# Short-convolution input projection in groups of four column tiles, half of the contraction by seven products of quarters

## The chip, the core and the metric

The kernel runs on one core of a Trainium2 chip. The metric is the device time of one execution, in microseconds (us); the median of three runs is given, and one further execution was taken with the hardware profiler. Engines are named as in the profile: PE is TensorE (matmuls; PEld its weight loads), DVE is VectorE, ACT is ScalarE, POOL is GpSimd, SP is SyncE, which here issues the loads from HBM.

## What is computed

Two layers over 512 latent tokens of width 1024: a mixer and a gated feed-forward part in each, with an adaptive normalisation ahead of both. The part that the change touches is the mixer of the second layer, a short gated convolution; the feed-forward part is shown because its up projection already has the form that the change uses.

```python
def short_conv_mixer(h, w_in, conv_w, conv_b, w_out):
    gate_b, gate_c, u = jnp.split(h @ w_in, 3, axis=-1)
    return (gate_b * dwconv3(gate_c * u, conv_w, conv_b)) @ w_out

def conv_ffn(h, w_up, conv_w, conv_b, w_down):
    a, val = jnp.split(h @ w_up, 2, axis=-1)
    return (jax.nn.gelu(dwconv3(a, conv_w, conv_b), approximate=False) * val) @ w_down

def dwconv3(h, w, b):
    hp = jnp.pad(h, ((0, 0), (1, 1), (0, 0)))
    return hp[:, :-2] * w[0] + hp[:, 1:-1] * w[1] + hp[:, 2:] * w[2] + b
```

`w_in` is 1024 x 3072, so the three outputs `gate_b`, `gate_c` and `u` have 8 column tiles of 128 each, 24 tiles.

## The kernel before

**Layout and precision.** Activations lie transposed: 128 features on the partitions, 512 tokens along the row, 8 such k tiles for a width of 1024. Each fp32 number is used as a high part (a cast to fp32r) and a low part (the rest). ACT casts the high part (`whi`), DVE subtracts it to get the low part (`wlo`), and each product is three matmuls (`mm3`, lines 288 to 290): high by high, high by the activation's low, low by high. One matmul multiplies a 128 x 128 weight block with 512 tokens ("wide") or with half of them ("narrow", 256).

**Weights.** `Weights` holds a plan of loads and of the blocks that are cast from each. `_load` (line 64) gives SP a load of 1 MB into one of two raw buffers `wraw`; `conv` casts the next block in the plan with ACT and DVE (lines 92 and 93, in `_block` lines 125 and 126). The cast blocks rotate through three buffers of 1024 columns, `whi` and `wlo`, so a block waits until the matmuls that read its buffer before are through.

**Quad and pair.** `quad` makes four tiles in two halves of 256 tokens, so that it can start when only the first half of the normalised activations is ready; after the first half's fourth k tile it calls `rest`, which finishes the norm. `pair` makes two tiles with 48 wide matmuls (8 k tiles, 3 each). The mixer's input projection takes a quad for the first c and u tiles and then pairs: b0, c1, u1, b1, c2, and so on to b3, ten pairs. After each pair ACT and DVE do the elementwise part: `cs` is a copy of c (line 1287), c times u (line 1295), the three taps by `conv3` (one ACT product, line 1212, and two DVE operations, lines 1213 and 1214), the product with b (line 1305), and the split into high and low (`mch`, `mcl`, lines 284 and 285) for the output projection `o1`.

**Group.** `group` makes four tiles in the up projections. The contraction's first half (k tiles 0 to 3), the four tiles and the 512 tokens are cut into quarters, and seven products of quarters take the place of eight: the quarters' sums and differences of the weights are made by DVE (`S1` to `S4`, lines 108 to 114), those of the activations once for each projection in `differences` (`T1` to `T4`, lines 1128 to 1138). Products: S1, A11, A12, S2, S3, S4 and A22, 12 narrow matmuls each. The second half of the contraction is done as before with W1 and W2, 24 wide matmuls each. In all 48 wide and 84 narrow. The sum of the products is made in PSUM and, between banks, by copies on ACT (line 1176) and additions on DVE (lines 1181 and 1201). The order of the casts is `QORDER`. S1 and A11 share one `whi`/`wlo` buffer, A12 has one, W1 one, then S2 with S3, S4 with A22, and W2 take the three again. The casts of S1, A11 and A12 of the next group are called behind W2's, that of W1 when the next group has started.

**Units.** The modulation of the second layer (a 1024 x 6144 product with one vector) is done on DVE between the other work: a unit is one `scalar_tensor_tensor` of 128 x 512 on a tile `ar` that SP has loaded (lines 485, 502, 504); after eight units come a reduction (line 508), two small matmuls that gather (`pad`, line 514), and four writes into `mod` (line 520). Three `ar` buffers rotate.

**Order.** The code is written in program order; a scheduler sets each engine's own order at build time, and each engine then takes its instructions strictly in that order, waiting on semaphores. Instructions marked with `pin` (the units among them) keep their order among themselves.

Of the kernel before, what the change touches and what calls it, by code (L numbers as in the profile page):

```python
# [9 lines left out]
F32 = mybir.dt.float32  # L10
# [8 lines left out]
P = 128  # L19
D = 1024  # L20
# [154 lines left out]
def backbone(ctx: ExitStack, tc: tile.TileContext, a, out, dump=None):  # L175
# [23 lines left out]
    def cols(w, c0):  # L199
        return [([ktiled(w)[:, :, c0 : c0 + 256]], [(0, 0, w.shape[0] // P, j, j + P) for j in (0, P)])]  # L200
# [20 lines left out]
    for j in range(4):  # L221
        plan += cols(w_out, 256 * j)

    def ffn_up_plan(l):
        r = cols(up[l], 0) + cols(up[l], FF)
        for j in range(FT // 2 - 1):
            q = [a["upq"][l, j, i][:, None, :] for i in range(2)]
            r += [([q[0]], QORDER), ([q[1]], [])]
        return r

    plan += ffn_up_plan(0)
    for j in range(4):
        plan += [rows_cols(down[0], k0, k1, 256 * j) for k0, k1 in kgroups]
    for j in range(4):
        plan += cols(od_in, D + 256 * j) + cols(od_in, 2 * D + 256 * j) + cols(od_in, 256 * j)
    for j in range(4):
        plan += cols(od_out, 256 * j)
    plan += ffn_up_plan(1)
# [856 lines left out]
    def pair(nm, src):  # L1095

        w = [ws.get(), ws.get()]
        o = [acc_t(f"pp{nm}{i}") for i in range(2)]
        for i in range(2):
            mms(o[i], w[i], src, 0, 0, KT, slice(0, T), True, True)  # L1100
        return o
# [121 lines left out]
    def units(n):  # L1223
        for _ in range(n):
            ada.unit(aux_t)
# [48 lines left out]
        dbg(f"xb{k}", xT[k][:])  # L1274


    mix = []
    for j in range(4):
        if j == 0:
            oc, ou = quad("c", nrm.h, rest)  # L1280
        else:
            oc = pair(f"c{j}", nrm.h)
            units(3)
        cs = []
        for i in range(2):
            t = gp.tile([P, T], F32, tag=f"g{16 + i}", name=f"cs{j}{i}")
            S.copy(t[:], oc[i][:])
            cs.append(t)
        if j:
            ou = pair(f"u{j}", nrm.h)  # L1290
            units(3)
        ts_ = []
        for i in range(2):
            m = 2 * j + i
            V.tensor_tensor(cs[i][:], ou[i][:], cs[i][:], ALU.mult)
            t = fp.tile([P, T], F32, tag="t", name=f"sc{m}", bufs=5)
            conv3(t, cs[i], rowv(76 + m, 1), rowv(84 + m, 1), rowv(92 + m, 1), rowv(68 + m, 1))
            ts_.append(t)
        ob = pair(f"b{j}", nrm.h)
        units(3)  # L1300
        for i in range(2):
            m = 2 * j + i
            mh = gp.tile([P, T], F32R, tag=f"g{2 * m}", name=f"mch{m}")
            ml = gp.tile([P, T], F32R, tag=f"g{2 * m + 1}", name=f"mcl{m}")
            V.tensor_tensor(ob[i][:], ob[i][:], ts_[i][:], ALU.mult)
            split(mh[:], ml[:], ob[i][:])
            mix.append((mh, ml))
    nrm = Norm("f1", 4, (1, 24))
    rest = project_back("o1", mix, [(0, 8)], mod[:, 1, 16:24], nrm)
    for k in range(KT):  # L1310
# [69 lines left out]
_INS = ["ada_w", "ev_w_in", "ev_w_out", "od_w_in", "od_w_out", "ffn_w_up", "ffn_w_down", "final_norm_w"]  # L1380


def layout(inputs):
    arrays = {n: np.ascontiguousarray(inputs[n]) for n in _INS}
    arrays["xT"] = np.ascontiguousarray(np.asarray(inputs["x"])[0].T)
# [2 lines left out]
                                "od_conv_w", "ada_b")]  # L1388
    for l in range(2):
        vecs += [inputs["ffn_conv_w"][l], inputs["ffn_conv_b"][l]]  # L1390
    q = np.asarray(inputs["ffn_w_up"]).reshape(2, KT, P, 2, FT // 2, 2, P)[:, :, :, :, 1:]
    blk = lambda k0, k1, m: q[:, k0:k1, :, :, :, m].transpose(0, 4, 2, 3, 1, 5).reshape(2, FT // 2 - 1, P, -1)
    arrays["upq"] = np.ascontiguousarray(np.stack([
        np.concatenate([blk(0, 2, 1), blk(2, 4, 1), blk(0, 2, 0), blk(2, 4, 0)], -1),
        np.concatenate([blk(4, 8, 0), blk(4, 8, 1)], -1)], 2))
    arrays["vec"] = np.ascontiguousarray(np.concatenate([np.asarray(v).reshape(-1, P) for v in vecs], 0).T)
    rpb = np.asarray(inputs["na_rpb"])[0].reshape(4, 2, 15, 31)
    rp = np.zeros((4, 15, 2, WPAD), rpb.dtype)
# [29 lines left out]
```

## Time and profile before

| | us |
|---|---|
| median of 3 runs | 1335.97 (1333.49 to 1336.93) |
| profiled execution, its own time | 1333.99 |
| its span, first to last instruction | 1332.2 |
| PE, DVE, ACT busy | 1304.5, 965.4, 625.2 |

The span is what the trace shows; 1.8 us of the execution lie around it. A row of the timeline reads: start, duration, engine, line, operation, tile written and tiles read, shape, number, and in brackets how long the engine had been idle before and what ended that. A matmul's duration is longer than the distance to the next one, as they are pipelined; the distance of the starts is what a stream of them costs. The same holds to a small degree for DVE and ACT.

### The profile page before, as it was taken

The numbers are of one execution on the slowest core, as the hardware profiler recorded it, in microseconds if no ns is written. First come the engines' busy times: TensorE is split into PE (matmuls) and PEld (weight loads), VectorE is DVE, ScalarE is ACT, GpSimd is POOL, SyncE is SP. The second block draws the span as 40 slices with busy tenths as digits, with TensorE's granted clock in tenths as the row PEclk, the third lists the DMA queues.
The fourth block names the chain that finished last, engine by engine and source line by source line (L and its number), as shares of the span: only waits on it lengthen the run. The fifth ranks groups of instructions, "written<-read, shape, count | busy, mean of one in ns | idle before, by whom it ended". The sixth has DMA issues, their size and how long they took to land. (4 is left out here: it accounts for less than half of the span.)

```text
span 1332.2 us, 21229 instructions
## 1 busy us (share of the span) xinstructions
PE 1304.5 (98%) x8456; PEld 1147.6 (86%) x8456; DVE 965.4 (72%) x1688; ACT 625.2 (47%) x1085; POOL 84.3 (6%) x87
## 2 busy tenths in 40 slices
PE   7999999999999999999999999999999999999997
PEld 4798888888779998889877898888999989899997
DVE  4668897887778878788766776667789897782333
ACT  4443445555545656565422253223456565663223
POOL 2204332311000000000000000000000000000000
PEclk9999999999999999999999999999999999999999
DMA  9842113674562122323466734555403423242231
GB/s 293 265 123 84 33 33 82 152 182 134 153 206 96 64 99 92 127 71 119 141 211 198 226 132 143 167 165 174 158 27 117 142 80 127 80 146 69 91 108 64
DMA packets 134995, 172.35 MB, mean 129 GB/s; under 512 B 14320, under 2 KB 103792, under 8 KB 129776
## 3 DMA queue, kind: packets, MB, share of 16 engines
q1 hardware_dynamic: 132896, 166.15, 39.3%
q10 hardware_dynamic: 2000, 4.85, 1.4%
q8 instruction: 66, 1.08, 0.3%
q14 instruction: 33, 0.27, 0.1%
HBM read 165.21 MB, written 2.10 MB: 126 GB/s over the span
## 5 line engine op out<-in xcount | busy, mean ns | idle before, releaser
L92 ACT CAST whi<-wraw 128x1024 fp32r<-128x1024 f32 (+1 forms) x122 | 124.1, 1021 | 280.8 <-PE pd L1340 70.4
L93 DVE TENSOR_TENSOR wlo<-wraw,whi 128x1024 fp32r<-128x1024 f32 (+1 forms) x122 | 145.2, 1192 | 107.7 <-ACT whi L92 107.1
L288 PE MATMUL p<-hf,whi 128*128 128x512 f32 (+1 forms) x640 | 215.4, 338 | 1.4 <-ACT whi L125 1.4
L290 PE MATMUL p<-hf,wlo 128*128 128x512 f32 (+1 forms) x640 | 214.6, 335 | 0.0
L289 PE MATMUL p<-hf,whi 128*128 128x512 f32 (+1 forms) x640 | 214.1, 335 | 0.0
L125 ACT CAST whi<-wraw 128x512 fp32r<-128x512 f32 (+1 forms) x160 | 113.0, 727 | 85.0 <-PE p L289 35.0
L290 PEld LDWEIGHTS p<-hf,wlo 128*128 128x128 f32 x640 | 120.1, 188 | 13.6
L288 PEld LDWEIGHTS p<-hf,whi 128*128 128x128 f32 x640 | 120.1, 188 | 12.3 <-ACT whi L125 1.6
L289 PEld LDWEIGHTS p<-hf,whi 128*128 128x128 f32 x640 | 120.1, 188 | 10.7
L126 DVE TENSOR_TENSOR wlo<-wraw,whi 128x512 fp32r<-128x512 f32 (+1 forms) x160 | 128.1, 817 | 0.9 <-ACT whi L125 0.5
L504 DVE SCALAR_TENSOR_TENSOR aa<-ar,sil,aa 128x512 f32<-128x512 f32 x140 | 104.8, 749 | 24.1 <-DMA ar<-in_ada_w_dram 21.8
L1339 PE MATMUL pd<-whi,g 128*128 128x256 f32 x352 | 98.2, 279 | 0.0
L1341 PE MATMUL pd<-wlo,g 128*128 128x256 f32 x352 | 98.1, 279 | 0.0
L1340 PE MATMUL pd<-whi,g 128*128 128x256 f32 x352 | 97.9, 278 | 0.0
L288 PE MATMUL pbd<-g,whi 128*128 128x512 f32 (+1 forms) x192 | 73.5, 383 | 0.0
L289 PE MATMUL pbd<-g,whi 128*128 128x512 f32 (+1 forms) x192 | 73.3, 382 | 0.0
L290 PE MATMUL pbd<-g,wlo 128*128 128x512 f32 (+1 forms) x192 | 73.1, 381 | 0.0
L288 PE MATMUL p<-T,whi 128*128 128x256 f32 x240 | 69.0, 288 | 0.0
L290 PE MATMUL p<-T,wlo 128*128 128x256 f32 x240 | 67.2, 280 | 0.0
L289 PE MATMUL p<-T,whi 128*128 128x256 f32 x240 | 67.2, 280 | 0.0
L1340 PEld LDWEIGHTS pd<-whi,g 128*128 128x128 f32 x352 | 66.3, 188 | 0.0
L1339 PEld LDWEIGHTS pd<-whi,g 128*128 128x128 f32 x352 | 66.1, 188 | 0.0
(679 smaller groups left out, 3296.3 us busy)
## 6 DMA issues: line engine op xcount, KB each, us to landing
ar<-in_ada_w_dram SPq DMA_DIRECT2D x160, 256.0 KB, 3.1
wraw<-in_upq_dram SPq DMA_DIRECT2D x40, 1024.0 KB, 4.8
wraw<-in_ffn_w_down_dram SPq DMA_DIRECT2D x16, 1024.0 KB, 5.3
wraw<-in_od_w_in_dram SPq DMA_DIRECT2D x12, 1024.0 KB, 5.6
wraw<-in_ev_w_in_dram SPq DMA_DIRECT2D x20, 512.0 KB, 5.2
araw<-in_ada_w_dram SPq DMA_DIRECT2D x16, 512.0 KB, 6.3
wraw<-in_ffn_w_down_dram SPq DMA_DIRECT2D x8, 768.0 KB, 4.7
wraw<-in_ev_w_out_dram SPq DMA_DIRECT2D x4, 1024.0 KB, 6.9
```

Of the source, the lines that this page charges most:

```text
L92: self.nc.scalar.copy(hv, rv)
L93: self.pin(self.nc.vector.tensor_tensor(lv, rv, hv.bitcast(F32), ALU.subtract))
L125: self.nc.scalar.copy(hi, src)
L126: V.tensor_tensor(lo, src, hi.bitcast(F32), ALU.subtract)
L288: TE.matmul(o, wh, mh, start=start, stop=False, skip_group_check=True)
L289: TE.matmul(o, wh, ml, start=False, stop=False, skip_group_check=True)
L290: TE.matmul(o, wl, mh, start=False, stop=stop, skip_group_check=True)
L504: pin(V.scalar_tensor_tensor(self.acc[:], raw[:], sil[:, r, 0:1], self.acc[:], ALU.mult, ALU.add))
L1339: TE.matmul(o[i][:, 0:256], gh[:, ts], w[0][:, k - k0], start=k == 0, stop=False)
L1340: TE.matmul(o[i][:, 0:256], gl[:, ts], w[0][:, k - k0], start=False, stop=False)
L1341: TE.matmul(o[i][:, 0:256], gh[:, ts], w[1][:, k - k0], start=False, stop=k == FT - 1)
```

## The change

The 20 tiles behind the quad are made by five groups in place of ten pairs. The quad makes c and u tiles 0 and 1 as before. Group 0 makes c and u tiles 2 and 3, group 1 the b tiles 0 to 3 (a gate group), groups 2 and 3 c and u of 4, 5 and 6, 7, and group 4 the b tiles 4 to 7. The convolved tiles `sc` now wait in buffers of their own for the gate group that needs them. `differences` runs within the quad, behind the norm's `rest`. The weights of the groups come from a new array `odq`, laid out beforehand as quarters. Units are called four times after the quad and three times after each half of a group.

```diff
+    def quarters(w):
+        return [([w[0][:, None, :]], QORDER), ([w[1][:, None, :]], [])]
...
-    for j in range(4):
-        plan += cols(od_in, D + 256 * j) + cols(od_in, 2 * D + 256 * j) + cols(od_in, 256 * j)
+    plan += cols(od_in, D) + cols(od_in, 2 * D)
+    plan += [e for j in range(5) for e in quarters(a["odq"][j])]
...
-    mix = []
-    for j in range(4):
-        if j == 0:
-            oc, ou = quad("c", nrm.h, rest)
-        else:
-            oc = pair(f"c{j}", nrm.h)
+    ts_, mv, mix = {}, [], {}
+
+    def short(m, c, u):
+        V.tensor_tensor(c[:], u[:], c[:], ALU.mult)
+        ts_[m] = gp.tile([P, T], F32, tag=f"g{16 + m}", name=f"sc{m}")
+        conv3(ts_[m], c, rowv(76 + m, 1), rowv(84 + m, 1), rowv(92 + m, 1), rowv(68 + m, 1))
+
+    def before():
+        rest()
+        mv.extend(differences("m", nrm.h))
+
+    oc, ou = quad("c", nrm.h, before, lambda: mv[1]())
+    for i in range(2):
+        t = fp.tile([P, T], F32, tag="t", name=f"cs{i}", bufs=5)
+        S.copy(t[:], oc[i][:])
+        short(i, t, ou[i])
+    units(4)
+    for n, js in enumerate(((1,), (0, 1), (2,), (3,), (2, 3))):
+        for i, (r0, r1) in enumerate(group(f"m{n}", mv[0])):
+            if len(js) == 1:
+                short(2 * js[0] + i, r0, r1)
+            else:
+                for j, r in zip(js, (r0, r1)):
+                    m = 2 * j + i
+                    V.tensor_tensor(r[:], r[:], ts_[m][:], ALU.mult)
+                    mix[m] = [gp.tile([P, T], F32R, tag=f"g{2 * m + z}", name=f"mc{m}{z}")[:] for z in range(2)]
+                    split(*mix[m], r[:])
             units(3)
-        cs = []
...
-        if j:
-            ou = pair(f"u{j}", nrm.h)
-            units(3)
...
-        ob = pair(f"b{j}", nrm.h)
-        units(3)
...
+def quarter_rows(w, a1, b1, a2, b2):
+
+    blk = lambda k0, k1, *t: w[k0:k1][:, :, list(t)].transpose(1, 2, 0, 3).reshape(P, -1)
+    return np.stack([np.concatenate([blk(0, 2, a2, b2), blk(2, 4, a2, b2), blk(0, 2, a1, b1), blk(2, 4, a1, b1)], 1),
+                     np.concatenate([blk(4, 8, a1, b1), blk(4, 8, a2, b2)], 1)])
...
+    q = np.asarray(inputs["od_w_in"])[0].reshape(KT, P, 24, P)
+    arrays["odq"] = np.ascontiguousarray(np.stack([quarter_rows(q, *t) for t in (
+        (10, 18, 11, 19), (0, 2, 1, 3), (12, 20, 13, 21), (14, 22, 15, 23), (4, 6, 5, 7))]))
```

Line numbers in the changed kernel are one lower than before up to the mixer (L503 is the unit of L504). Where the engines' orders change, at the two places of which the prediction speaks:

DVE before, around the cast of a weight block between two pairs (`aa` is the unit's sum, `wlo` a weight low, `cs` c times u, `sc` a tap):

```order
L504 SCALAR_TENSOR_TENSOR aa_8646<-ar_8644,sil,aa_8646 128x512
L1295 TENSOR_TENSOR cs_8580<-ppu_8594,cs_8580 128x512
L93 TENSOR_TENSOR wlo_8667<-wraw_8513,whi_8666 128x1024
L1213 SCALAR_TENSOR_TENSOR sc_8657<-cs_8580,vec,sc_8657 128x511
L1214 SCALAR_TENSOR_TENSOR sc_8657<-cs_8580,vec,sc_8657 128x511
L1295 TENSOR_TENSOR cs_8582<-ppu_8595,cs_8582 128x512
```

DVE after, the last rows of the stretch from W2's low of group 2 to W1's low of group 3 (`wlo_8868` is S1 and A11, `wlo_8886` A12, `wlo_8944` W1; `Rm2r` and `Rm2t` are sums of group 2's second half):

```order
L503 SCALAR_TENSOR_TENSOR aa_8706<-ar_8699,sil,aa_8706 128x512
L126 TENSOR_TENSOR wlo_8868<-wraw_8812,whi_8867 128x512
L503 SCALAR_TENSOR_TENSOR aa_8706<-ar_8704,sil,aa_8706 128x512
L503 SCALAR_TENSOR_TENSOR aa_8706<-ar_8851,sil,aa_8706 128x512
L126 TENSOR_TENSOR wlo_8886<-wraw_8812,whi_8885 128x512
L1180 TENSOR_TENSOR Rm2r_8714<-p10m_8710,Rm2r_8714 128x256
L1180 TENSOR_TENSOR Rm2t_8715<-p11m_8711,Rm2t_8715 128x256
L503 SCALAR_TENSOR_TENSOR aa_8706<-ar_8856,sil,aa_8706 128x512
L1279 TENSOR_TENSOR Rm2r_8714<-Rm2t_8715,Rm2r_8714 128x512
L503 SCALAR_TENSOR_TENSOR aa_8706<-ar_8859,sil,aa_8706 128x512
L126 TENSOR_TENSOR wlo_8944<-wraw_8862,whi_8943 128x1024
```

Five units now stand in the queue ahead of W1's low, among the four lows that the next group needs, where before there was one wide low to a pair.

DVE after, behind the quad (`cs` and `sc` as above, `wlo_8249` is A12, `wlo_8253` W1):

```order
L1279 TENSOR_TENSOR cs_8208<-ppc_7934,cs_8208 128x512
L1279 TENSOR_TENSOR cs_8215<-ppc_7935,cs_8215 128x512
L1212 SCALAR_TENSOR_TENSOR sc_8211<-cs_8208,vec,sc_8211 128x511
L1213 SCALAR_TENSOR_TENSOR sc_8211<-cs_8208,vec,sc_8211 128x511
L1212 SCALAR_TENSOR_TENSOR sc_8218<-cs_8215,vec,sc_8218 128x511
L1213 SCALAR_TENSOR_TENSOR sc_8218<-cs_8215,vec,sc_8218 128x511
L503 SCALAR_TENSOR_TENSOR aa_7723<-ar_7716,sil,aa_7723 128x512
L126 TENSOR_TENSOR wlo_8249<-wraw_7773,whi_8248 128x512
L503 SCALAR_TENSOR_TENSOR aa_7723<-ar_7721,sil,aa_7723 128x512
L126 TENSOR_TENSOR wlo_8253<-wraw_8197,whi_8252 128x1024
```

PE after, at A12's turn in group 0 (`whi_8248` is A12, `whi_8283` S2 with S3, `p00m` to `p11m` the four banks):

```order
L289 MATMUL p11m_8243<-hm_6912,wlo_8203 128x256
L287 MATMUL p00m_8240<-hm_6913,whi_8248 128x256
L288 MATMUL p00m_8240<-hm_6913,whi_8248 128x256
L287 MATMUL p01m_8241<-hm_6913,whi_8248 128x256
L287 MATMUL p10m_8242<-Tm_8032,whi_8283 128x256
L287 MATMUL p11m_8243<-Tm_8032,whi_8283 128x256
L289 MATMUL p00m_8240<-hm_6913,wlo_8249 128x256
```

There, where the pair's first matmul stood right behind the quad's last, PE now has eight matmuls with high parts (two for each bank) and then the first that needs A12's low.

## Rows read from the trace of the kernel before

**Rows 1.** The page, busy us, share of the span and instructions of each engine.
```profile
PE 1304.5 (98%) x8456; PEld 1147.6 (86%) x8456; DVE 965.4 (72%) x1688; ACT 625.2 (47%) x1085; POOL 84.3 (6%) x87
```
**Rows 2.** Table of stretches: length, busy of PE, PEld, DVE, ACT, POOL; clock, DMA, GB/s.
```profile
806.34:917.14 110.80, 110.80 (x490) 91.06 (x489) 75.76 (x109) 34.40 (x43) 0.00 (x0) 1.00 0.54 170
525.96:547.04 21.08, 21.08 (x133) 19.00 (x132) 16.76 (x28) 12.44 (x24) 0.00 (x0) 1.00 0.27 100
1027.88:1049.05 21.17, 21.17 (x135) 19.09 (x134) 18.98 (x35) 12.20 (x24) 0.00 (x0) 1.00 0.37 125
...
669.10:672.40 3.30, 3.30 (x10) 2.52 (x9) 3.17 (x7) 0.00 (x0) 0.00 (x0) 0.50 0.56 176
```
**Rows 3.** Timeline of PE: wide, narrow, and a gather.
```profile
806.34 0.39 PE L288 MATMUL ppb<-hm,whi 128*128 128x512 f32 x1
806.56 0.39 PE L289 MATMUL ppb<-hm,whi 128*128 128x512 f32 x1
...
525.96 0.28 PE L288 MATMUL p<-hf,whi 128*128 128x256 f32 x1
526.08 0.28 PE L289 MATMUL p<-hf,whi 128*128 128x256 f32 x1
...
1027.74 0.29 PE L514 MATMUL pad<-ad,cst 128*128 128x16 f32 x2
```
**Rows 4.** Timeline of DVE from a group's W2 low to the next W1 low.
```profile
1040.57 1.22 DVE L126 TENSOR_TENSOR wlo<-wraw,whi 128x1024 fp32r<-128x1024 f32 x1
1041.70 0.42 DVE L1181 TENSOR_TENSOR R13t<-p,R13t 128x256 f32<-128x256 f32 x1
1042.03 0.68 DVE L1201 TENSOR_TENSOR R13sqa<-p,R13sqa 128x512 f32<-128x512 f32 x1
1042.63 0.68 DVE L1201 TENSOR_TENSOR R13t<-p,R13t 128x512 f32<-128x512 f32 x1
...
1050.72 1.22 DVE L126 TENSOR_TENSOR wlo<-wraw,whi 128x1024 fp32r<-128x1024 f32 x1
```
**Rows 5.** Timeline of DVE: a mod write, a unit, the low behind it.
```profile
1033.95 0.14 DVE L520 TENSOR_TENSOR mod<-pad,vec 32x4 f32<-32x4 f32 x1
...
1034.73 0.74 DVE L504 SCALAR_TENSOR_TENSOR aa<-ar,sil,aa 128x512 f32<-128x512 f32 x1
1035.39 0.68 DVE L126 TENSOR_TENSOR wlo<-wraw,whi 128x512 fp32r<-128x512 f32 x1
```
**Rows 6.** Timeline around the ends of two quads, the last up projection's and this stage's.
```profile
982.87 0.69 DVE L285 TENSOR_TENSOR T<-df,T 128x512 fp32r<-128x512 f32 x1
...
985.00 0.28 PE L288 MATMUL p<-hf,whi 128*128 128x256 f32 x1
...
987.26 0.36 PE L288 MATMUL p<-hf,whi 128*128 128x256 f32 x1 [0.74 <-ACT whi L125]
...
805.50 1.07 ACT L1287 COPY cs<-ppc 128x512 f32<-128x512 f32 x2 [8.92 <-PE ppc L290]
...
806.27 1.29 DVE L1295 TENSOR_TENSOR cs<-ppc,cs 128x512 f32<-128x512 f32 x2 [7.90 <-PE ppc L290]
```
**Rows 7.** Timeline of ACT: two tap products, W1's cast, a bank copy.
```profile
984.23 1.45 ACT L1212 ACTIVATE cv<-ppa,vec 128x512 f32<-128x512 f32 x2 [1.39 <-PE ppa L290]
...
1049.59 1.05 ACT L125 CAST whi<-wraw 128x1024 fp32r<-128x1024 f32 x1
1050.66 0.37 ACT L1176 COPY R14t<-p 128x256 f32<-128x256 f32 x1
```
**Rows 8.** Timeline of PE behind two idle stretches.
```profile
668.45 0.40 PE L514 MATMUL pad<-ad,cst 128*128 128x16 f32 x2 [1.91 <-DVE ad L508]
...
354.37 0.50 PE L288 MATMUL pg<-h,whi 128*128 128x512 f32 x1 [1.33 <-ACT vn L852]
```
**Rows 9.** Timeline of DVE, a unit that waits for its DMA.
```profile
766.26 0.75 DVE L504 SCALAR_TENSOR_TENSOR aa<-ar,sil,aa 128x512 f32<-128x512 f32 x1 [1.96 <-DMA ar<-in_ada_w_dram]
```
**Rows 10.** DMA issues: tile, engine, number, KB each, median us to landing.
```profile
ar<-in_ada_w_dram SPq DMA_DIRECT2D x160, 256.0 KB, 3.1
```

More of the change, by code (lines that the diff above doesn't have):

```diff
@@ L222, in backbone @@
         plan += cols(w_out, 256 * j)
+    def quarters(w):
+        return [([w[0][:, None, :]], QORDER), ([w[1][:, None, :]], [])]
     def ffn_up_plan(l):
[L225 to L229, printed above, removed]
+        return cols(up[l], 0) + cols(up[l], FF) + [e for j in range(FT // 2 - 1) for e in quarters(a["upq"][l, j])]
     plan += ffn_up_plan(0)
@@ L1274, in backbone @@
         dbg(f"xb{k}", xT[k][:])
-    mix = []
-    for j in range(4):
-        if j == 0:
-            oc, ou = quad("c", nrm.h, rest)
-        else:
-            oc = pair(f"c{j}", nrm.h)
-            units(3)
-        cs = []
[L1285 to L1288, printed above, removed]
-        if j:
-            ou = pair(f"u{j}", nrm.h)
-            units(3)
[L1292 to L1298, printed above, removed]
-        ob = pair(f"b{j}", nrm.h)
-        units(3)
[L1301 to L1307, printed above, removed]
+    ts_, mv, mix = {}, [], {}
[22 more added lines that the diff above has]
+                    split(*mix[m], r[:])
+            units(3)
     nrm = Norm("f1", 4, (1, 24))
@@ L1390, in layout @@
         vecs += [inputs["ffn_conv_w"][l], inputs["ffn_conv_b"][l]]
[L1391 to L1395, printed above, removed]
+    q = np.asarray(inputs["ffn_w_up"]).reshape(2, KT, P, 2 * FT, P)
+    arrays["upq"] = np.ascontiguousarray(np.stack([np.stack([
+        quarter_rows(q[l], f, FT + f, f + 1, FT + f + 1) for f in range(2, FT, 2)]) for l in range(2)]))
+    q = np.asarray(inputs["od_w_in"])[0].reshape(KT, P, 24, P)
+    arrays["odq"] = np.ascontiguousarray(np.stack([quarter_rows(q, *t) for t in (
+        (10, 18, 11, 19), (0, 2, 1, 3), (12, 20, 13, 21), (14, 22, 15, 23), (4, 6, 5, 7))]))
     arrays["vec"] = np.ascontiguousarray(np.concatenate([np.asarray(v).reshape(-1, P) for v in vecs], 0).T)
```

## The prediction

> **What bounds the kernel now.** The page's busy times come first [rows 1]: TensorE (PE) is busy 98% of the span, VectorE (DVE) 72%, ScalarE (ACT) 47%. The table of stretches then shows the stage that changes [rows 2]: from 806.34 to 917.14 us, 110.80 us, PE is busy all the time at clock 1.00, and DVE has 35 us idle. So this stage is priced by counting matmuls. The same table has two groups of the up projections, the form that the stage is to take: 21.08 us with 16.76 us of DVE work in a group without units, 21.17 and 18.98 in one with two. PE is full there too, but DVE has only 4.3 and 2.2 us left. That margin is what I read closest.
>
> **What PE saves.** Wide matmuls start 0.22 to 0.23 us apart (the stage's 480 take 0.229 each), narrow ones 0.12 [rows 3]. Four tiles by pairs are 96 wide: 96 x 0.229 = 21.98. A group is 48 wide and 84 narrow: 10.99 + 84 x 0.117 = 20.82; measured, with what changing width costs, 21.08 [rows 2]. Five groups are 105.4. A gather pair takes 0.14 us to the next start and makes that one longer, 0.2 together [rows 3]; four fall in the stage: 106.2. Against 110.80 that is **4.6 us at most**, 0.34%. Weight bytes and the quad stay as they are, and units up to the output projection become 34 for 30. The differences of the activations are new in this stage, DVE and ACT work under the quad. The up projection has the same chain in the same place, and its last low ends at 983.56, 1.4 us before the first product behind the quad starts at 985.00 [rows 6]; this stage's quad has the same matmuls, so I cost the chain at nothing, and at what it comes later if DVE is more than 1.4 us behind.
>
> **Where DVE stands between a group and the next.** Each group casts W2 late, since W2 takes the buffer in which W1 lies until its products are through; then DVE must finish adds, the tiles' arithmetic and the lows of S1, A11, A12 and W1 of the next group. In the trace of before [rows 4] W2's low ends at 1041.79 and the next W1 low at 1051.94: 10.15 us of queue without a hole, 7.26 of them before the next group starts at 1049.05 [rows 2], so W1's low is there 2.89 us into the group. In the new order PE wants it after 24 matmuls of S1 and A11, 6 of A12 and two wide high ones: 30 x 0.117 + 0.46 = 3.97 us in. Slack: 1.08 us.
>
> Now the same stretch in the new order (the first pair of listings), with start-to-start times: 0.60 for a 512-wide subtract, add or multiply, 0.335 for 256, 1.13 for 1024 [rows 4], 0.66 for a unit or a tap (both scalar_tensor_tensor), 0.14 for a mod write [rows 5]; the reduce I count as a unit. Against the 10.15 us, the stretch from group 2 to group 3 gains two products of the tiles (1.2), five units (3.3) and four mod writes (0.55), and loses a multiply, a low of g, S2's sum and one tap, which now lie behind W1 or are gone (2.5): 12.7 us. From group 1 to 2, a gate group, it is 12.25 by the same count (four multiplies, two lows of mix, an add and three units more; three taps, a multiply, a low of g and S2's sum less). From 0 to 1 it is 11.5; from 3 to 4 12.0.
>
> W2's low ends 7.4 to 7.6 us before the next group starts, where PE doesn't wait between. So W1's low would come 4.9 us into group 2 and 5.1 into group 3, where 3.97 is wanted: **stalls of 0.9 and 1.1 us**. In group 1 it comes at 4.1, with a gather ahead of it (need 4.2): none. In group 3 the wait stands ahead of both W1 products, DVE's work behind W1's low is only 6 us, and W2's low ends 9.0 us before group 4 starts: none there. One unit more or less in such a stretch is 0.66 us.
>
> **The first group** has no lead at all. In the trace PE waits 0.74 us in this place of the up projection [rows 6]. In the new order (the second pair of listings), counted from the quad's end, 806.34 in the trace of before: ACT's copies of the two c tiles end at 0.2 and DVE starts its two multiplies at -0.1 [rows 6]; the first tap waits for ACT's tap product and starts at 1.5; four taps and the mod writes carry DVE to 4.45, a unit to 5.1, and only then A12's low ends at 5.8; another unit and W1's low follow to 7.6. PE has done S1 and A11 at 3.0 (a gather, 24 x 0.117) and then has eight high matmuls (0.9 us), which wait in pieces for ACT: two tap products (0.73 each), W1's cast (1.05) and four bank copies (0.37) [rows 7], with two casts between, end at 5.3. So PE is idle for 5.8 - 3.0 - 0.9, about **1.85 us**, and afterwards W1, S2 and S3 come in time (S2's low at 8.8, wanted at 9.9).
>
> **Behind the last group.** When its W2 is through, DVE has two adds, a weight low, two units, a reduce and two multiplies ahead of mix tiles 5 and 7: high parts 4.9 and 5.5 us, low parts 5.6 and 6.2 us after the group. In the new order of PE 15 matmuls of the first output tile and 7 of the second stand ahead of them (5.2 us): nothing is lost, or 0.5 at most. Four units leave the last up projection, two groups less with units: 2 x 0.09 [rows 2], at most 0.2 us gained; I take 0.1.
>
> **Sum.** Groups 0 to 4: 105.4, gathers 0.8, stalls 1.85 + 0.9 + 1.1 = 3.85: 110.05, against 110.80. Gain 0.75, with the 0.1 behind it 0.85. The profiled execution took 1333.99 us (1332.2 of span), so 1333.1 of it; the median of the runs shown is 2.0 us higher, 1335.97, and becomes **1335.2 us** (rounded up, since nothing is taken for late handovers). The stalls are what is unknown: none, if the lows come early everywhere, or twice as much, if a cast or a DMA is late too: 106.2 to 113.9, a gain of 4.7 to a loss of 3.0.
>
> **A rule against it.** A 512-wide low takes 0.68 us and the next starts 0.60 after it; a 1024-wide one takes 1.22, and 1.13 [rows 4, 5]. So two narrow ones cost 0.07 more than a wide one, which the measured groups have in them. The Trainium skill, "VectorE: DVE Perf Modes", section "The TRN2 errata", says that each SBUF operation pays a fixed latency, so that many small tiles pay it many times; its (N + 151)/0.96 gives an estimate of 691 and 1224 ns. The durations agree with it, the spacing doesn't; by it a pair of narrow lows would cost 0.16 more than a wide one, and the five groups together some 1.5 us more than by the rows.
>
> **Rivals.**
> (a) No stall: DVE is early everywhere. For it: PE lost under 0.1 us in groups with two units [rows 2]. Against: the sums above exceed the slack. 1335.97 - 4.7 = 1331.3. Chance 0.10.
> (b) The clock falls in group 0. PE idled 1.91 us before 668.45, and the stretch 669.1 to 672.4 ran at 0.50, the lower level of 1.2 GHz [rows 2, 8]; after 1.33 us before 354.37 there was no such stretch near. My 1.85 us are broken by eight matmuls. Half the clock for 3.3 us loses 1.65: 1336.8. Chance 0.22.
> (c) Slower: a unit in front of W1's low waits for its own DMA. In the down projection DVE stood 1.96 us before one unit [rows 9], and everything behind it in the queue too. Such a wait in each of the five groups, with the slack used up, is 9.8 us: 1345. It decides from the first wait over 0.1 us in groups 2 and 3. Against it: the stage moves 170 GB/s and the new one no more [rows 2], a column lands 3.1 us after issue [rows 10], and with three buffers over 4 us lie between a unit and the one that reuses its buffer. Chance 0.10.
> (d) DVE operations hold the engine for their whole duration, 0.08 us more each: some 20 in the stretch, 1.6 us in each of four groups, 1335.2 + 6.4 = 1341.6. [rows 4] show 0.60 where the duration is 0.68. Chance 0.03. That each operation costs the full figure is what the Trainium skill's section named above would have, its formula read as spacing.
> The forecast keeps 0.55.
>
> **How the numbers follow.** The bound for no change is 0.3%, 4 us, about what a measurement can tell. Faster than 1332.0: (a), 0.10. Slower than 1340.0: (c) and (d), 0.13. Within: 0.77. The range goes from (a), 1331.3, over (b) and the doubled stalls (1335.2 + 3.85) to 1339.0, and leaves out (c) and (d).
>
> **What would show it.** In the new trace the stage from the quad's end to the first matmul of the output projection is about 110 us. PE waits some 1.9 us in pieces within 6 us after the quad, with ACT copies and then DVE (A12's low) named; in groups 2 and 3 it waits about 1 us, some 4 us into the group, for the 1024-wide low; groups 1 and 4 are near 21.3 us. DVE's idle time lies behind W1's low, not ahead of it. Wrong would be: five groups at 21.1 (then DVE's queue was never late), units that wait for DMA (c), or a stretch at 0.50 (b).

## The result, and where the time went

The changed kernel takes 1341.22 us (median of 5 runs, 1340.04 to 1341.73) against 1335.97: a ratio of 1.0044, 95% interval 1.0034 to 1.0055. It is slower, by more than a measurement's uncertainty, where the forecast was 1335.2 and the range ended at 1339.0.

The table of stretches of the kernel after, made as [rows 2] (length; busy us of PE, PEld, DVE, ACT, POOL with their instructions; granted clock, DMA share, GB/s). Its rows are the stage, its five groups, the output projection, and the down projection of layer 0:

```profile
808.41:919.82 111.41, 107.86 (x669) 95.19 (x668) 103.71 (x176) 53.08 (x100) 0.00 (x0) 1.00 0.50 161
808.41:831.76 23.35, 21.86 (x135) 19.25 (x134) 20.84 (x36) 10.84 (x21) 0.00 (x0) 1.00 0.41 136
831.76:853.29 21.53, 21.53 (x136) 19.03 (x134) 20.86 (x37) 10.65 (x21) 0.00 (x0) 1.00 0.56 184
853.29:875.11 21.82, 21.66 (x135) 19.11 (x134) 20.66 (x38) 10.35 (x20) 0.00 (x0) 1.00 0.49 159
875.11:898.24 23.13, 21.51 (x136) 18.89 (x134) 21.08 (x34) 10.64 (x20) 0.00 (x0) 1.00 0.51 162
898.24:919.82 21.58, 21.29 (x135) 18.92 (x134) 20.27 (x36) 10.61 (x20) 0.00 (x0) 1.00 0.54 167
919.82:964.66 44.84, 42.15 (x216) 35.18 (x214) 36.49 (x60) 17.27 (x22) 0.00 (x0) 1.00 0.66 220
653.55:781.42 127.87, 123.48 (x560) 101.24 (x558) 89.35 (x136) 32.96 (x38) 0.00 (x0) 0.97 0.67 217
```

The same table of the kernel before, of its output and down projections:

```profile
917.14:958.20 41.06, 41.06 (x213) 34.85 (x212) 30.28 (x43) 16.53 (x20) 0.00 (x0) 1.00 0.60 196
652.46:779.64 127.18, 123.46 (x559) 101.27 (x558) 87.98 (x134) 33.06 (x38) 0.00 (x0) 0.97 0.68 217
```

Two things stand there. The stage is no shorter than the 110.80 us of [rows 2], although PE's busy time in it fell by 2.9: DVE, 75.76 us busy before, now has 103.71 of 111.41, and PE waits for it. And the output projection, whose code was not touched, takes 44.84 us where it took 41.06. The profiled spans, 1339.4 and 1332.2, differ by 7.2: stage with the gather in front of it 0.75, output projection 3.8, the up projection behind it 0.65, 1.8 before the quad of the stage, where the order of work did not change, and 0.2 in smaller pieces. The 1.8 lies within the spread of the runs: over the traces of before, after and the runs e2 to e5, with the same order up to there, the down projection starts at 652.5 to 654.5 us and takes from 125.2 to 129.3 us.

In the stage the longest wait is in group 3, for W1's low. Timeline of PE, then of DVE in front of it (start, duration, line, tiles, in brackets the idle time before and what ended it):

```profile
880.90 0.50 PE L289 MATMUL p01m<-hm,wlo 128*128 128x512 f32 x1 [1.62 <-DVE wlo L126]
```
```profile
866.41 1.21 DVE L126 TENSOR_TENSOR wlo<-wraw,whi 128x1024 fp32r<-128x1024 f32 x1
...
867.87 0.68 DVE L1200 TENSOR_TENSOR Rm2sqa<-p00m,Rm2sqa 128x512 f32<-128x512 f32 x1
868.47 0.68 DVE L1200 TENSOR_TENSOR Rm2t<-p01m,Rm2t 128x512 f32<-128x512 f32 x1
869.07 0.14 DVE L519 TENSOR_TENSOR mod<-pad,vec 32x4 f32<-32x4 f32 x1
869.18 0.69 DVE L1279 TENSOR_TENSOR Rm2sqa<-Rm2t,Rm2sqa 128x512 f32<-128x512 f32 x1
869.91 0.33 DVE L519 TENSOR_TENSOR mod<-pad,vec 32x4 f32<-32x4 f32 x2
870.26 0.69 DVE L108 TENSOR_TENSOR ws<-wraw 128x512 f32<-128x512 f32 x1
870.99 0.17 DVE L519 TENSOR_TENSOR mod<-pad,vec 32x4 f32<-32x4 f32 x1
871.19 0.75 DVE L1212 SCALAR_TENSOR_TENSOR sc<-Rm2sqa,vec,sc 128x511 f32<-128x511 f32 x1
...
877.70 0.74 DVE L503 SCALAR_TENSOR_TENSOR aa<-ar,sil,aa 128x512 f32<-128x512 f32 x1
878.36 0.69 DVE L1279 TENSOR_TENSOR Rm2r<-Rm2t,Rm2r 128x512 f32<-128x512 f32 x1
878.96 0.75 DVE L503 SCALAR_TENSOR_TENSOR aa<-ar,sil,aa 128x512 f32<-128x512 f32 x1
879.63 1.22 DVE L126 TENSOR_TENSOR wlo<-wraw,whi 128x1024 fp32r<-128x1024 f32 x1
```

The queue runs without a hole from W2's low to W1's, which ends 5.73 us into the group. Of the five units in it the last two stand right ahead of W1's low.

The output projection, DVE and then PE:

```profile
930.22 2.33 DVE L503 SCALAR_TENSOR_TENSOR aa<-ar,sil,aa 128x512 f32<-128x512 f32 x3
...
937.47 0.75 DVE L503 SCALAR_TENSOR_TENSOR aa<-ar,sil,aa 128x512 f32<-128x512 f32 x1 [3.79 <-DMA ar<-in_ada_w_dram]
...
941.98 0.70 DVE L507 TRANSPOSE_TENSOR_REDUCE ad<-aa 128x16 f32<-128x512 f32 x1
```
```profile
942.74 0.40 PE L513 MATMUL pad<-ad,cst 128*128 128x16 f32 x2 [1.47 <-DVE ad L507]
...
961.87 0.38 PE L287 MATMUL pbo<-mc,whi 128*128 128x256 f32 x1 [0.82 <-DVE xT L1001]
...
964.66 0.45 PE L1013 MATMUL pnf<-sqaf,ones 128*128 128x256 f32 x1 [0.40 <-DVE sqaf L1009]
```

DVE stands 3.79 us before a unit whose own load has not landed. PE, in order, reaches the gather of that run of eight, whose reduce (941.98) comes behind this unit and the next, and waits 1.47 us; further on it waits twice more for DVE. The queue of SyncE shows how late the load went out:

```profile
926.68 2.27 SPq L484 DMA_DIRECT2D ar<-in_ada_w_dram  x3
930.17 0.38 SPq L63 DMA_DIRECT2D wraw<-in_od_w_out_dram  x1
931.00 7.58 SPq L484 DMA_DIRECT2D ar<-in_ada_w_dram  x4
```

A unit's load goes out when DVE has used the buffer. DVE came out of the stage with adds, multiplies and splits of two tiles still to do, so the stage's last three units came only at 926.18 to 928.60, and the first three of the output projection (930.22) directly behind. The fourth, at 937.47, has its load issued at 931.00, right behind a weight slab of 1 MB (930.17). It landed 6.4 us after issue (3.1 is the median of [rows 10]). That is no exception in this trace: the 17 of the 160 unit loads that went out within 1 us behind a weight slab took 4.5 to 8.0 us, the 26 that went out with no other load under way 2.7 in the median and 3.5 at most.

### The profile page after: what moved, and what is told of

It is laid out like the page before. It is cut to its first block, busy times and chain, and to the rows that moved or that the text cites. A ratio compares the mean times of both kernels' runs of the same rounds, so it can differ in the third digit from the quotient of the medians.

```text
span 1339.4 us, 21783 instructions
## 1 busy us (share of the span) xinstructions
PE 1303.6 (97%) x8636; PEld 1152.4 (86%) x8636; DVE 1005.6 (75%) x1780; ACT 647.1 (48%) x1149; POOL 84.5 (6%) x87
## 5 line engine op out<-in xcount | busy, mean ns | idle before, releaser
L92 ACT CAST whi<-wraw 128x1024 fp32r<-128x1024 f32 (+1 forms) x102 | 103.0, 1015 | 211.9 <-PE pd L1336 70.4
L125 ACT CAST whi<-wraw 128x512 fp32r<-128x512 f32 x200 | 141.4, 728 | 115.5 <-PE p L288 35.1
L93 DVE TENSOR_TENSOR wlo<-wraw,whi 128x1024 fp32r<-128x1024 f32 (+1 forms) x102 | 120.9, 1188 | 91.9 <-ACT whi L92 91.5
L126 DVE TENSOR_TENSOR wlo<-wraw,whi 128x512 fp32r<-128x512 f32 x200 | 160.5, 817 | 3.4 <-ACT whi L125 1.9
L287 PEld LDWEIGHTS p<-hf,whi 128*128 128x128 f32 x640 | 120.1, 188 | 12.7 <-ACT whi L125 1.6
L503 DVE SCALAR_TENSOR_TENSOR aa<-ar,sil,aa 128x512 f32<-128x512 f32 x140 | 104.7, 748 | 30.1 <-DMA ar<-in_ada_w_dram 28.5
```

Of the source, the lines that this page charges most:

```text
L92: self.nc.scalar.copy(hv, rv)
L93: self.pin(self.nc.vector.tensor_tensor(lv, rv, hv.bitcast(F32), ALU.subtract))
L125: self.nc.scalar.copy(hi, src)
L126: V.tensor_tensor(lo, src, hi.bitcast(F32), ALU.subtract)
L287: TE.matmul(o, wh, mh, start=start, stop=False, skip_group_check=True)
L503: pin(V.scalar_tensor_tensor(self.acc[:], raw[:], sil[:, r, 0:1], self.acc[:], ALU.mult, ALU.add))
```

## Experiments

Theory U: the units of the modulation in DVE's queue ahead of lows cost the stage its gain, and the same units delay the output projection. Rival F: the groups' own taps, adds and splits do it, with or without units.

**e1_moved** takes all units out of the stage.

```diff
                 gated_tile(2 * j + i, ra, rv)
+                if l == 0 and i == 0 and j < 9:
+                    units(4)
...
-    units(4)
+    units(0)
...
-            units(3)
+            units(0)
```

> The changed kernel with no units in the stage (34 go): 32 of them run in the up projection of layer 0 instead, four behind the first yield of each of groups 1 to 8, ahead of the W2 low. Theory U (the units stand in VectorE's queue ahead of the lows; that is the stage's stalls and the late output projection): groups 1 to 4 at 21.1 us, group 0 about 22.2 (its taps still stand ahead of A12's low), the stage about 106.6 against 111.55; the output projection comes back by 2 to 4 us; up projection of layer 0 at most 2 us longer (eight gathers at 0.2). Together 1334 to 1336. Rival F (the groups' own adds, taps and splits make VectorE late, units or not): the stage stays above 110 and the time at 1340 to 1343.

Measured: 1347.49 us, ratio 1.0082 (1.0062 to 1.0102). The total was missed by 12 us, the stage hit to 0.15: its table of stretches (stage, groups 0, 1 and 2, and 222 us of the first up projection, where the units now are):

```profile
820.81:927.27 106.46, 105.98 (x664) 94.37 (x663) 81.67 (x133) 53.62 (x99) 0.00 (x0) 1.00 0.29 99
820.81:842.43 21.62, 21.14 (x136) 19.05 (x135) 18.23 (x33) 11.08 (x21) 0.00 (x0) 1.00 0.28 98
842.43:863.66 21.23, 21.23 (x134) 18.82 (x132) 15.80 (x27) 10.85 (x20) 0.00 (x0) 1.00 0.29 100
863.66:884.83 21.17, 21.17 (x134) 18.89 (x133) 16.52 (x28) 10.57 (x20) 0.00 (x0) 1.00 0.28 100
...
442.90:664.90 222.00, 212.69 (x1319) 189.52 (x1318) 192.40 (x325) 124.47 (x231) 0.00 (x0) 0.99 0.40 133
```

So without units the groups do save nearly what PE's count said (106.46 against 110.80), and F falls: there is 0.5 us of waiting left. But four units a group, given out behind the first yield, made the first up projection 224.1 us long where it took 211.4, 9.3 us of it waiting (222.00 - 212.69): in DVE's order three or four of them came to stand behind W2's low, ahead of the next W1 low. "Behind the first yield" in the code was no place ahead of W2's low in the queue. PE's waits there are another path than in the stage: 7.9 of the 9.3 us are for ACT's copies of a bank (L1175), and ACT itself stood 9.6 us, in ten waits, ahead of its gelu (L1234) for DVE's last tap (L1213), which now came behind units; in the changed kernel ACT does not wait there.

**e4_first_half** tried that place in the stage itself.

```diff
-            units(3)
+            units(6 if i == 0 else 0)
```

> The changed kernel with the same 34 units, but all six of a group behind its first yield (ahead of W2's low, where VectorE waits for TensorE anyway) and none behind the second. Theory U, in the form that the place counts: the stretch from W2's low to the next W1 low shortens by 3 x 0.66 = 2.0 us, so that groups 2, 3 and 4 lose their stalls (0.5, 1.85 and 0.5) and the output projection starts with VectorE 2 us less late: 1341.2 - 2.9 - 1.5 = 1336.8. Rival S (VectorE is simply full, 16.76 + 6 x 0.66 = 20.7 of 21.1 us a group, the place counts for nothing): W2's low comes late instead and the time stays at 1340 to 1342.

Measured: 1348.99 us, ratio 1.0098 (1.0079 to 1.0117), the stage 119.86 us. It did not do what it was meant to: in the order that came out, 4, 6, 5 and 4 units stand between W2's low and W1's in groups 1 to 4, where 3, 3, 5 and 3 had stood. As a test of the place in the code it says nothing, but it shows what more units ahead of W1's low do: PE waits 4.3 us in four waits for W1's low, 2.1 in the changed kernel. With six, group 2 takes 26.74 us, and this is its wait and what follows it (timeline of PE, table of stretches):

```profile
863.47 0.79 PE L289 MATMUL p01m<-hm,wlo 128*128 128x512 f32 x1 [2.48 <-DVE wlo L126]
```
```profile
863.47:869.70 6.23, 6.23 (x18) 5.17 (x19) 4.88 (x11) 2.23 (x4) 0.00 (x0) 0.50 0.01 4
```

Behind 2.48 us of idling PE runs at 0.50, 1.2 GHz; the trace has this level from 862.9 to 869.7, so an estimated 3.1 us of the stage's 119.86, half of the 6.23 of that row, are the clock and not waits. Behind the 1.62 us in the changed kernel's group 3 the table above has 1.00.

**e3_quad_none** leaves the four units behind the quad out, so that the others move up.

```diff
-    units(4)
+    units(0)
```

> The changed kernel without the four units behind the quad (30 units in the stage, as many as before; the output projection's units then have the same place in their run of eight as before). Theory U: A12's low and W1's low of group 0 come 0.7 and 1.3 us earlier, group 0 goes from 23.5 to about 22.4; if it is the phase of the units that made the output projection late, another 3 us come back there: 1337 with it, 1340.1 without it. Rival F: group 0 within 0.3 us of 23.5 (taps and copies hold A12's low), 1341.

Measured: 1340.59 us, ratio 1.0036 (1.0023 to 1.0050). Group 0 came to 21.66 us, like the 21.62 of e1 and less than expected: the units there cost 1.7 us, more than the 1.3 of two units; I did not take that apart. But the units behind moved: 5, 4, 3 and 3 stand ahead of W1's low, group 1 takes 23.0 and group 2 24.7, and the stage 112.53. Group 2 has a stretch at 0.50 in it, behind two shorter pieces of idling (timeline of PE, table of stretches):

```profile
855.28 0.39 PE L287 MATMUL p00m<-hm,whi 128*128 128x256 f32 x1 [1.07 <-ACT Rm2r L1175]
857.27 0.69 PE L289 MATMUL p00m<-hm,wlo 128*128 128x512 f32 x1 [0.56 <-DVE wlo L126]
```
```profile
857.40:860.80 3.40, 3.40 (x9) 2.64 (x10) 3.40 (x6) 1.14 (x2) 0.00 (x0) 0.50 0.62 163
```

Half the clock for 3.4 us is an estimated 1.7 us of the 24.7. The output projection stayed at 44.1: the phase of the units alone does not decide there.

**e2_o1_one** gives the first two steps of the output projection one unit each instead of four.

```diff
-                units(4 if len(groups) == 1 else 5)
+                units((1 if nm == "o1" else 4) if len(groups) == 1 else 5)
```

> The changed kernel with one unit instead of four ahead of each of the first two steps of the output projection (the other six run in the last up projection). Theory U: the 3.79 us that VectorE stood before a unit for its DMA at 937.47 is gone, TensorE's 1.47 us at 942.7 and most of the 0.82 and 0.40 us at 962 to 965 with it: 1341.2 - 2.5 = 1338.7, the stage unchanged at 111.5. Rival F: the output projection is late because the last group's adds and splits are, and stays within 0.7 us: 1340.5 to 1341.5.

Measured: 1338.36 us, ratio 1.0025 (1.0011 to 1.0038), as U had it, and still slower than the kernel before. The stage is unchanged, the output projection 2.9 us shorter:

```profile
806.72:918.12 111.40, 107.77 (x670) 95.15 (x668) 103.58 (x175) 53.05 (x100) 0.00 (x0) 1.00 0.50 161
918.12:960.08 41.96, 41.61 (x214) 35.00 (x212) 31.22 (x47) 17.38 (x22) 0.00 (x0) 1.00 0.59 196
```

**e11_no_loads** keeps every unit and its place, and takes away only the loads.

```diff
+            if 59 <= n < 113 or 148 <= n < 156:
+                self.raw[n] = self.raw[n - 1]
+                return
```

> The changed kernel with the DMAs of units 59 to 112 (the first down projection's) and 148 to 155 (the output projection's) left out: these units read the slab that lies in the buffer, so the modulation is computed from other numbers; all other work and its order stay. Theory D (VectorE waits for the units' own loads, and TensorE behind it for the gather in its queue): the output projection goes from 44.8 to 41.5 us, the down projection from 127.9 to 120, in which no gather waits and the clock stays at 1.00; the stage unchanged at 111.4; 1341.2 - 8 - 3 = 1330. Rival B (twelve units in a row are too much work for VectorE there, loads or not): the output projection stays above 44.

Measured: 1329.51 us, ratio 0.9957 (0.9941 to 0.9973). Stage, output projection, down projection:

```profile
800.08:911.46 111.38, 107.70 (x670) 95.07 (x668) 103.65 (x175) 53.12 (x100) 0.00 (x0) 1.00 0.49 161
911.46:953.26 41.80, 41.73 (x216) 35.13 (x214) 36.72 (x60) 17.20 (x22) 0.00 (x0) 1.00 0.56 189
652.96:773.19 120.23, 120.08 (x560) 98.99 (x559) 88.92 (x136) 33.09 (x38) 0.00 (x0) 1.00 0.34 113
```

The output projection has the same 60 DVE instructions, 36.72 us of them, as in the changed kernel, and takes 41.80 us. So it is the wait for the load that costs 3 us there, not the amount of DVE work; rival B falls. The down projection loses its 4 us of waits and its stretch at 0.50 with the loads. The stage is as it was: there the units cost by their work.

**e5_mid** gives six units out in the middle of each group, and none elsewhere in the stage.

```diff
         copy(1, A, 0, B)
+        mid()
         upto(9)
...
-    units(4)
+    units(0)
-        for i, (r0, r1) in enumerate(group(f"m{n}", mv[0])):
+        for i, (r0, r1) in enumerate(group(f"m{n}", mv[0], lambda: units(6))):
...
-            units(3)
+            units(0)
```

> The changed kernel with 30 units in the stage, six given out in the middle of each group (behind the copies of the second bank) and none behind the quad or the yields. In VectorE's queue 2, 3, 2 and 3 units then stand between W2's low and the next W1 low of groups 1 to 4, where 3, 3, 5 and 3 stood. Theory Q (each unit in that stretch makes W1's low 0.66 us later, others cost nothing there): group 3 falls from 23.1 to about 21.3, groups 1, 2 and 4 stay at 21.2 to 21.8, group 0 at 21.7 as in the run without units: the stage 107.7 against 111.4; the output projection, with 11 units in it, stays late by 2 to 3 us: 1337 to 1338. Rival S (VectorE is full, only the number of units counts): the stage at 110 to 111, 1340.

Measured: 1337.21 us, ratio 1.0014 (1.0005 to 1.0023). The total fits Q, its reasons do not. The stage stayed at 111.64 (S was right on that): DVE's W1 lows came early, at 2.7 to 3.6 us into groups 1 to 4, but PE waited elsewhere, 1.1 us for the first cast of a group, 0.7 for a narrow low, and 0.5 and 0.4 for the adds of the first yield. What got shorter was the output projection, 41.04 us with all its eight units: three units of the stage, not six, stand behind the last W2 low, and the longest wait of a unit for its load is 0.7 us.

**e6_spread, e8_before_spread.** Twenty units in the stage: e6 has the lines of e5 with 4 in place of 6, e8 the kernel before with `units(2)` in place of its `units(3)`. Both have the call of `mid()` and these lines:

```diff
-                units(4 if len(groups) == 1 else 5)
+                units((1 if nm == "o1" else 4) if len(groups) == 1 else 5)
...
-            for i, (ra, rv) in enumerate(group(f"{l}{j}", mv[0])):
+            for i, (ra, rv) in enumerate(group(f"{l}{j}", mv[0], lambda: units(2 if l == 0 else 2) if j < 9 else None)):
-            if l and j < 9:
-                units(2)
```

> The changed kernel with the units spread: two in the middle of each group 1 to 8 of the first up projection (16 more there), four in the middle of each of the stage's groups (20 in place of 34; 0, 1, 0 and 1 of them between W2's low and the next W1 low), one in place of four in each of the first two steps of the output projection. Theory Q: the stage at 106.9 (group 0 21.7, the others 21.2 with a gather in half of them), the output projection within 1 us of the 41.1 of the kernel before, the first up projection at most 1 us longer: 1335.7 - 3.9 + 0.5 + 0.7 = 1333, faster than both kernels. Rival F (the groups cost what they save): 1336 or more.

> The kernel before (pairs) with the same spreading: two units in the middle of each group 1 to 8 of the first up projection, two in place of three at each of the ten places of the stage, one in place of four in each of the first two steps of the output projection. Theory Q: pairs leave VectorE 35 us idle in the stage, so that nothing is gained there: stage 110.7, and 1335 to 1336.5, as before. If spreading by itself brings what e6_spread brings (the down projection or the output projection of the kernel before gain from it), it is under 1334.

Measured on the same chip: 1334.31 us (0.9997, 0.9988 to 1.0007) and 1335.39 us (0.9997, 0.9986 to 1.0008). Neither differs from the kernel before, and no difference between them is shown either. e8 came out as Q said, with the stage at 110.57 us; e6 missed by 1.3, since its stage took 109.36, not 106.9.

**e7_spread_d0, e9_before_d0.** The same two, with fewer units in each step of the down projection and more in the first up projection.

```diff
-                units((1 if nm == "o1" else 4) if len(groups) == 1 else 5)
+                units((2 if nm == "o1" else 4) if len(groups) == 1 else 4)
...
-lambda: units(2 if l == 0 else 2)
+lambda: units(3 if l == 0 else 2)
```

> The kernel of the run e6_spread with four in place of five units in each step of the first down projection and three in place of two in the middle of each group of the first up projection. There VectorE waits for units' DMAs in runs of five, and TensorE waits 2 us twice behind it. If the waits come from the rate of the runs: 1 to 3 us less than e6_spread, 1331; if the weights' own loads set it: the same as e6_spread.

> The kernel before (pairs) with the same spreading as the run e7_spread_d0 (three units in the middle of each group 1 to 8 of the first up projection, four in place of five in each step of the first down projection, two in place of three in the stage, two in place of four in the first two steps of the output projection). It tells what of e7_spread_d0's 1326.6 belongs to the groups. Theory Q: the down projection gains the same 7.5 us, the stage stays at 110.7 against 108.0 there, the output projection is about 1.5 us shorter than there: 1326.6 + 2.7 - 1.5 = 1327.8, 1 us behind it. Rival F (groups are worth nothing): 1326 or less.

Measured: e7 1326.55 us, ratio 0.9941 (0.9927 to 0.9955), faster than both kernels and 7.8 us less than e6 where 1 to 3 were expected; e9 1329.44 us, 0.9961 (0.9946 to 0.9975), 1.6 more than expected. Most of e7's gain lies in the down projection, 119.68 us where it took 127.18 (rows: stage, output projection, down projection):

```profile
799.24:907.21 107.97, 106.67 (x666) 94.88 (x665) 96.26 (x158) 54.01 (x99) 0.00 (x0) 1.00 0.41 145
907.35:949.76 42.41, 41.48 (x213) 34.56 (x212) 29.65 (x43) 17.40 (x22) 0.00 (x0) 1.00 0.53 178
652.82:772.50 119.68, 119.68 (x560) 99.26 (x559) 80.05 (x123) 32.84 (x38) 0.00 (x0) 1.00 0.64 206
```

No gather waits there and the clock is 1.00 throughout, as without loads. That has nothing to do with the groups, and e9 has it too: 120.21 us, in a profiled execution whose granted clock was 0.95 throughout, for which its stage is not compared here. The groups' own share would be the 2.9 us between e9 and e7, about the difference of the stages (110.57 by pairs in e8, 107.97). The intervals of the two ratios overlap, so that share is likely and not shown.

**e10_few, e12_three.** Ten and fifteen units in the stage; against e7, e10 first and then e12:

```diff
-lambda: units(3 if l == 0 else 2) if j < 9 else None
+lambda: units(4 if l == 0 else 2) if j < (9 if l else 11) else None
-group(f"m{n}", mv[0], lambda: units(4))
+group(f"m{n}", mv[0], lambda: units(2))
```
```diff
-units((2 if nm == "o1" else 4) if len(groups) == 1 else 4)
+units((1 if nm == "o1" else 4) if len(groups) == 1 else 4)
-lambda: units(3 if l == 0 else 2) if j < 9 else None
+lambda: units(3 if l == 0 else 2) if j < (9 if l else 11) else None
-group(f"m{n}", mv[0], lambda: units(4))
+group(f"m{n}", mv[0], lambda: units(3))
```

> The kernel of the run e7_spread_d0 with two in place of four units in the middle of each of the stage's groups (10 in the stage) and four in place of three in the middle of groups 1 to 10 of the first up projection. Third point of a series: the stage took 106.5 us with no unit, 108.0 and 109.4 with 20, 111.4 and 111.6 with 34 and 30. Theory Q (VectorE has room for two or three units a group): 107.0, and with the output projection as there 1325.5. If the stage's cost goes by the number alone, 0.15 us each: 108.0 and no change, 1326.6. The first up projection, with four in each group, shows it again: under 0.2 us a group longer by Q.

> The changed kernel with three units in the middle of every group of the first up projection (groups 1 to 10) and of the stage, four in place of five in each step of the first down projection and one in place of four in the first two steps of the output projection. In VectorE's queue no unit then stands between a W2 low and the next W1 low, in either place. Theory Q (three units a group fit behind W1's low, one ahead of it costs a stall, a fourth makes W2's low late): groups 1 to 4 of the stage at 21.1 to 21.3, group 0 at 21.7, the stage 107.0; the first up projection within 0.6 us of the kernel before; the output projection 41: 1325.5, faster than e7_spread_d0's 1326.6 by about 1. Rival (the units cost by number wherever they stand, 0.15 us each): the stage 108.7, 1327 to 1328.

Measured: e10 1330.74 us (0.9967, 0.9956 to 0.9977), e12 1327.46 us (0.9947, 0.9934 to 0.9960). e10 lost what it gained: its stage was near Q's 107.0, but four units in each of ten groups made the first up projection longer, 217.3 us where the kernel before took 211.4, 0.6 a group and not under 0.2. e12 is level with e7, and its stage of 108.94 is the rival's 108.7, not Q's 107.0. The series of the stage, with the units that stand in DVE's order between W2's low and the next W1 low of groups 1 to 4:

| kernel | units in the stage | ahead of W1's low | stage, us |
|---|---|---|---|
| e1 | 0 | 0, 0, 0, 0 | 106.46 |
| e10 | 10 | 0, 0, 1, 0 | 107.36 |
| e12 | 15 | 0, 0, 0, 0 | 108.94 |
| e7 | 20 | 0, 1, 0, 1 | 107.97 |
| e6 | 20 | 0, 1, 0, 1 | 109.36 |
| e5 | 30 | 2, 3, 2, 3 | 111.64 |
| e3 | 30 | 5, 4, 3, 3 | 112.53 |
| after | 34 | 3, 3, 5, 3 | 111.41 |
| e4 | 34 | 4, 6, 5, 4 | 119.86 |

Neither rule holds alone. The stage grows with the number of units up to 34, but not by a fixed price: e7 with 20 is below e12 with 15. The place stands out in e4, with as many units as the changed kernel; an estimated 1.7 us of e3 and 3.1 of e4 are the stretches at 0.50. e12 shows one thing that a unit does without standing ahead of W1's low at all. Timeline of DVE in its group 2, then of PE:

```profile
855.82 0.67 DVE L519 TENSOR_TENSOR mod<-pad,vec 32x4 f32<-32x4 f32 x4 [2.22 <-PE pad L513]
...
856.60 0.75 DVE L503 SCALAR_TENSOR_TENSOR aa<-ar,sil,aa 128x512 f32<-128x512 f32 x1
857.26 1.22 DVE L126 TENSOR_TENSOR wlo<-wraw,whi 128x1024 fp32r<-128x1024 f32 x1
858.51 0.42 DVE L1180 TENSOR_TENSOR Rm2r<-p10m,Rm2r 128x256 f32<-128x256 f32 x1
```
```profile
859.00 0.39 PE L287 MATMUL p10m<-Tm,whi 128*128 128x256 f32 x1 [0.27 <-DVE Rm2r L1180]
```

A finished run of eight waits on DVE for its gather on PE; a unit and W2's low follow, and the add that frees the bank for A22's product comes behind both. The wait that it ends is 0.27 us, of 2.5 by which e12's stage is longer than e1's. PE's other waits there are 0.5 for a weight low and 0.2 for another such add, beside 0.6 for an ACT copy, which e1 has too. What makes e6 1.4 us slower than e7 in the stage, with equal counts, I did not take apart.

## Why the prediction was wrong

- **Behind the last group: the step that failed.** It read "nothing is lost, or 0.5 at most" and lost 3.8 us. It followed the lows of the mix tiles to PE, for which PE indeed did not wait; it did not follow the units that stand in DVE's queue behind them, nor their loads in SyncE's queue behind the weight slab. e2, with fewer units there, brings 2.9 us back, and e11, with all units and without their loads, 3.0: the wait for the loads is shown as the cause of these. That the slab made the load late is read from the trace; no run moves the slab alone. The 0.7 to 0.9 us that e2 and e11 still have over the 41.06 of before were not taken apart.
- **Rival (c)** had the mechanism, a unit that waits for its own DMA with everything behind it, and the wrong place: in the stage no unit of the changed kernel waits 0.2 us for its load. Its argument against, that three buffers leave over 4 us, does not hold where units follow each other directly. Nor is the 3.1 us of [rows 10] the time of a load behind a slab: in the trace of before the 16 unit loads that went out within 1 us behind one took 4.5 to 8.3.
- **The stalls of the stage**, 3.85 us forecast, were 5.35 (111.55 with the gather in front, less 105.4 and 0.8). By group, what they have over 21.08 and a gather: group 0 2.2 for 1.85 (A12's low came 6.2 us after the quad, not 5.8), group 1 0.25 for none, group 2 0.54 for 0.9, group 3 1.85 for 1.1, group 4 0.5 for none. The brackets hold only 3.55 us of it, PE's idle time in the stage. A wait costs more than its bracket: with 1.62 in brackets, the start at 880.90 comes 2.01 behind the one before it and 0.34 ahead of the next, where 0.23 is the distance in a stream. The mechanism, W1's low behind the units, was right; the worst term was W1's low of group 3, 5.73 us in and not 5.1. 0.37 of these 0.63 us are the mod writes, below. In group 4 the low came at 4.48, not 3.0, part of it 0.6 us in which DVE waited for the last products. The stretches from W2's low to the next W1 low took 11.4, 12.8, 13.2 and 13.5 us, where 11.5, 12.25, 12.7 and 12.0 were counted.
- **What PE saves** was right to about 0.1 us a group: 21.17 to 21.23 us for groups 1 to 4 of e1, 21.08 taken. e1's stage saves 4.3 us, but it has one gather in it where the 4.6 was worked out with four; without the three others the forecast's rule gives 5.2.
- **The last up projection** was to gain 0.1 and lost 0.65. PE has two waits in it that the kernel before has not, 0.3 us for a weight low and 0.2 for a bank copy; what made them was not looked into.
- **Sum**: 1335.2, and 1.5 more stall, 3.8 in the output projection and 0.75 in the last up projection are 1341.25; measured 1341.22. The sum of the parts holds; that it meets the median to 0.03 us is chance, since the runs spread over 1.7.
- **Rival (b)**: group 0 idled 1.48 us in three pieces and its clock stayed at 1.00. The fall appeared in the stage of e4, behind one wait of 2.48 us, and in that of e3, behind pieces of 1.07 and 0.56. So that the 1.85 us are broken by matmuls was no safe argument against it.
- **Rival (d)**: the two wide adds ahead of group 3's mod writes start 0.60 apart as in [rows 4], with durations of 0.68. The durations agree with the figure of the Trainium skill, "VectorE: DVE Perf Modes", section "The TRN2 errata", an estimate of 0.69 by its formula; read as spacing it does not hold here either.

## What to carry to other kernels

When a stage's bound moves from one full engine to another that is nearly full, all that was hidden on the second engine gets a price: count it by stretches between the handovers that the first engine waits for, and look at the queue that came out, not at the line of code where the work is given out. Follow filler work past the end of the stage, with its loads and with what it sends back to the other engine: here an untouched stage paid five times what the changed one did. A gain of 4 us was there in the stage; it needed the fillers elsewhere. Shorter runs of fillers and their loads, in the down projection, were worth more than the change.

## What the runs showed of the hardware

- Four adds of 32x4 out of PSUM, 0.14 to 0.17 us each, between 512-wide operations took 0.92 us of DVE's queue (869.07 to 871.19 holds two wide operations at 0.60 and the four), not the 0.55 that the prediction took from a row of one. The first of the four left the spacing as it was (0.60 behind the wide add, 0.11 to the next start); ahead of the second and of the fourth the wide operation held 0.73 in place of 0.60, and the last three took 0.17 to 0.20 each. Shortness alone is not the reason, then. In the code the four write to partitions that start at 0, 32, 64 and 96, so only the first starts where its neighbours do; whether that is the cause no run shows.
- A load of 256 KB issued 0.83 us behind one of 1 MB landed after 6.4 us, while DMA moved 220 GB/s over the output projection; the median of all 160 is 3.1, that of the 17 within 1 us behind a slab 6.3.
- PE's clock stayed at 1.00 behind idle stretches of 1.47 and 1.62 us in the changed kernel, and was 0.50 behind 2.48 us in e4 and behind 2.75 us in the down projection of the changed kernel (first row below). But the length of an idle stretch does not decide by itself: in e3 the clock stayed at 1.00 behind 3.19 us (second row, and 1.00 in the stretch from there to 706.00) and fell behind 1.07 and 0.56, and in e6 it stayed at 1.00 behind 2.03 before 702.57. What else decides, no run here shows.

```profile
702.97:708.50 5.53, 5.53 (x14) 4.29 (x13) 3.04 (x5) 1.05 (x1) 0.00 (x0) 0.50 0.65 199
```
```profile
702.11 0.37 PE L513 MATMUL pad<-ad,cst 128*128 128x16 f32 x2 [3.19 <-DVE ad L507]
```
